# Every projection of a two-block model: 512 tokens per TensorE product, or two products of 256

## The chip, the cores and the metric

The kernel runs on one core of one Trainium2 chip. The metric is device microseconds of one execution, from launch to the last output. TensorE (PE in the rows) multiplies a stationary operand that a weight load (PEld) brings in by a moving operand of up to 512 columns, and writes to PSUM; VectorE (DVE) and ScalarE (ACT) empty PSUM and prepare operands, GpSimd (POOL) does small side work, SyncE (SP) issues the large loads.

## The reference

A sequence of 512 tokens of width 1024 goes through two blocks, all in float32:

```python
h = h + hybrid_mixer(rmsnorm(h))          # block 1: w_in projections, SSD, window attention, w_out
h = h + hierarchical_moe(rmsnorm(h))      # 64 experts, two per token
h = rmsnorm(h)
h = h + hybrid_mixer_2(rmsnorm_2(h))      # block 2: w_in projections, neighbourhood attention, GLA, w_out
u = rmsnorm_2(h) @ w_ff1                  # 1024 -> 4096
h = h + jnp.square(jax.nn.relu(u)) @ w_ff2
```

What the change touches is every product of the normed activations by a 128-column slice of an input weight: `proj = h @ w_in` in both mixers (all but a few narrow columns), and `u = ... @ w1` in the last feed-forward.

## The kernel before

Activations lie transposed: `A` is a pair of tiles of 128 partitions x 8 x 512 (features, tokens). To keep float32 accuracy with a faster product, each operand is split in two parts, a rounded one (H) and the remainder (L), and three products stand for one: H by H, H by L, L by H. `mm3` (L174) issues them, L178, L179 and L180:

```python
m = mm(out, lH, rH, start=first, stop=False)
mm(out, lH, rL, start=False, stop=False)
mm(out, lL, rH, start=False, stop=last)
```

`wsplit` (L152) splits a 128-column slice of a weight: ScalarE copies it rounded (`wH`, L158), VectorE subtracts (`wL`, L159). `proj` (L191) then makes one output slice of 128 features x 512 tokens in one PSUM bank of the pair tagged `pj`: 8 steps over the features, three products each, 24 products of 512 tokens. The weight part is the stationary operand, the activations are the moving one. The parameter `cuts` makes it go over the tokens in pieces, and is 2 for the first two slices of the feed-forward only (L1697). `late` (L1387, the first two value slices of block 2) issues all products with `wH` first, and those with `wL` behind.

There are 86 projections: 30 in block 1 (10 in `attention1`, 4 in `ssd_head`, 16 in `ssd`), 24 in block 2 (4 values, two of them `late`, 8 queries and keys, 8 + 4 in `gla`), 32 in `ffn`. Each is followed by VectorE or ScalarE work that reads the whole bank. Output projections (`wout`, `wout_tail`) also use `mm3`, with the weights as moving operand of 512 columns; `proj` is not in them. Between the blocks the experts stream their weights through SP's queue (L149).

The kernel is built through a framework that schedules: it puts the instructions of each engine into one fixed order by priorities and by its own estimate of when each is ready, and adds the waits. So an edit can also change where other instructions stand.

Of the kernel before, what the change touches and what calls it, by code (L numbers as in the profile page):

```python
# [15 lines left out]
P = 128  # L16
T = 512
# [11 lines left out]
class Net:  # L29
# [158 lines left out]
                                  start=True, stop=True)  # L188
        self.copy(out, p)

    def proj(self, W, A, m=P, cuts=1, late=False):  # L191

        p = self.psum("pj")
        kt = W[0].shape[1]
        if late:
            for k in range(3 * kt):
                w, a = ((0, 0), (0, 1))[k % 2] if k < 2 * kt else (1, 0)
                k, n = (k // 2 if k < 2 * kt else k - 2 * kt), k
                self.nc.tensor.matmul(p[:m], W[w][:, k, :], A[a][:, k, :], start=n == 0, stop=n == 3 * kt - 1)
            return p  # L200
        for c in range(cuts):
            ts = slice(c * (T // cuts), (c + 1) * (T // cuts))
            for k in range(kt):
                self.mm3(p[:m, ts], (W[0][:, k, :], W[1][:, k, :]), (A[0][:, k, ts], A[1][:, k, ts]), k == 0, k == kt - 1)
        return p
# [1165 lines left out]
    def neighbours(self, small, pool, wp, mixp, w_in, A):  # L1371
# [6 lines left out]
        W = []  # L1378
# [5 lines left out]
        for j in range(4):  # L1384
            if j > 1:
                W.append(self.wsplit(wp, wv[j], P))
            p = self.proj(W[j], A, P, late=j < 2)  # L1387
            self.copy(bycol(vT[:, j, :]), raster(p))

        row = self.dram.tile([1, T], FT, name="r2d")  # L1390
# [77 lines left out]
        for j in range(4):  # L1468
            now, ahead = ahead, project(j + 1) if j < 3 else None
            if j == 0:  # L1470

                v = []
                for n in range(7):
                    p = self.psum("tp")
# [210 lines left out]
    def ffn(self, pool, wp, A, r3):  # L1685
        nc, i, h = self.nc, self.ins, self.H
        V = nc.vector
        w1 = i["w_ff1_2"][0].rearrange("(k p) n -> p k n", p=P)
        w2 = i["w_ff2_2"][0].rearrange("(k p) n -> p k n", p=P)
        for q in range(4):  # L1690
            mixes = []
            for b in range(2):
                w = self.ring([P, KT, 512], w1[:, :, (2 * q + b) * 512:(2 * q + b + 1) * 512])
                m = self.mixtile(pool)
                mixes.append(m)
                for j in range(4):
                    p = self.proj(self.wsplit(wp, w[:, :, j * P:(j + 1) * P], P), A, P, 2 if q + b == 0 and j < 2 else 1)  # L1697
                    r = pool.tile([P, T], FT, name="r", bufs=2)
                    nc.scalar.activation(r, p, AF.Relu)
                    s = pool.tile([P, T], FT, name="s", bufs=2)  # L1700
                    V.scalar_tensor_tensor(s, p, 0.0, r, op0=OP.max, op1=OP.mult)
                    self.split(m[0][:, j, :], m[1][:, j, :], s)
            w = [self.ring([P, 4, D], w2[:, 8 * q + 4 * b:8 * q + 4 * b + 4, :]) for b in range(2)]
            srcs = lambda half, s: w[s // 2][:, 2 * (s % 2):2 * (s % 2) + 2, half * 512:half * 512 + 512]
            if q < 3:
                self.wout(wp, h, srcs, mixes, r3)
            else:
                self.wout(wp, h, srcs, mixes[:1], r3)
                g = self.row(pool, "ln_final_g_2")
                out = self.out[0].rearrange("(c p) d -> p c d", p=P)  # L1710
                self.wout_tail(self.tail_weights(wp, self.halves(self.mixtile(pool)), w[1]), h, mixes[1], r3,
                               lambda c: nc.sync.dma_start(out[:, c, :], self.normed(pool, h[:, c, :], g)))
# [114 lines left out]
```

## Time and profile before

| | us |
|---|---|
| median of 3 runs | 2036.48 (2032.88 to 2038.64) |
| profiled execution | 2035.26 |
| its span, first to last instruction | 2033.5 |
| TensorE busy | 1936.5 (95%) |
| VectorE / ScalarE busy | 948.4 / 534.1 |
| mean granted TensorE clock | 0.985 of full |

The span divides into five stages: loads and the first norm (to about 20 us), the mixer of block 1 (to 362), the tail of block 1, routing and experts (to 1340), the mixer of block 2 (to 1670) and the feed-forward (to the end). A row of the trace of one product gives its start and how long it takes from start to end; products overlap, so the time that one costs TensorE is the distance from its start to the next one's start, called a step below.

### The profile page before, as it was taken

What the parts mean: (1) busy time and instruction counts of PE and PEld (TensorE: products, weight loads), DVE (VectorE), ACT (ScalarE), POOL (GpSimd) and SP (SyncE); (2) the same over time, 40 slices, a digit from 0 to 9 for tenths busy, and PEclk for the clock granted to TensorE, in tenths of its full rate; (3) what the DMA queues carried; (4) which work ended last, traced back from release to release, by engine and by line L of the source; (5) the groups of instructions that cost most, each with busy time, mean ns of one, the idle gap of its engine ahead of it and who ended that gap; (6) DMA issues with size and microseconds to landing.
All of it is one profiled execution on the core that took longest, in us unless ns stands there. A gap on an engine that the chain in (4) does not pass through costs nothing. (4 is left out here: it accounts for less than half of the span.)

```text
span 2033.5 us, 24005 instructions
## 1 busy us (share of the span) xinstructions
PE 1936.5 (95%) x9535; PEld 1217.1 (60%) x9535; DVE 948.4 (47%) x1891; ACT 534.1 (26%) x899; POOL 192.1 (9%) x245
## 2 busy tenths in 40 slices
PE   7999999999999899999999999999999999999998
PEld 6788777734444344334344434447777778888886
DVE  6764657743543244243244333235655664443355
ACT  5773445311000010010010010024442433232232
POOL 5210333110000000000000000002201110000000
PEclk9999999999999999999999999999999999999999
DMA  7312012799999999999999999984212112313211
GB/s 203 115 43 83 27 70 111 259 342 415 415 424 426 424 424 424 424 424 425 424 424 424 422 422 424 422 320 68 91 42 83 43 52 83 118 50 123 99 68 42
DMA packets 114777, 494.24 MB, mean 243 GB/s; under 512 B 16492, under 2 KB 23091, under 8 KB 74984
## 3 DMA queue, kind: packets, MB, share of 16 engines
q1 hardware_dynamic: 107720, 483.63, 59.8%
q0 software_dynamic: 6352, 6.96, 1.5%
q10 hardware_dynamic: 592, 2.10, 0.3%
q8 instruction: 76, 1.25, 0.2%
q14 instruction: 37, 0.30, 0.0%
HBM read 500.68 MB, written 6.15 MB: 249 GB/s over the span
## 5 line engine op out<-in xcount | busy, mean ns | idle before, releaser
L986 PE MATMUL pj<-w,xg 128*64 128x512 f32 x1696 | 470.1, 608 | 45.9 <-DMA w<-in_w_up 45.2
L986 PEld LDWEIGHTS pj<-w,xg 128*64 128x64 f32 x1696 | 154.8, 140 | 332.2 <-issue 255.0
L159 DVE TENSOR_TENSOR wL<-w,wH 128x1024 fp32r<-128x1024 f32 x135 | 167.0, 1237 | 205.4 <-ACT wH L158 203.0
L158 ACT CAST wH<-w 128x1024 fp32r<-128x1024 f32 x136 | 142.4, 1048 | 343.4 <-PE pj L179 169.4
L1091 DVE SCALAR_TENSOR_TENSOR hid<-pj,slots,hid 128x512 f32<-128x512 f32 x30 | 22.5, 751 | 430.1 <-PE pj L986 415.8
L1190 DVE TENSOR_TENSOR H<-sc,H 128x512 f32<-128x512 f32 x248 | 156.6, 683 | 6.2 <-PE sc L1187 3.5
L986 PE MATMUL pj<-w16x,xg 128*64 128x512 f32 x352 | 151.7, 614 | 1.1 <-DMA w16x<-in_w_gate 1.1
L1187 PE MATMUL sc<-yH,ST 128*128 128x512 f32 x256 | 112.8, 441 | 0.6 <-DVE H L1190 0.6
L843 POOL DMA_INDIRECT rows<-hd,tok x31 | 31.7, 1022 | 815.1 <-DVE gates L837 576.3
L1100 ACT COPY hT<-tp 128x512 f32<-128x512 f32 x32 | 18.8, 587 | 339.8 <-PE tp L1098 339.8
L180 PE MATMUL pj<-n3H,wL 128*128 128x512 f32 (+1 forms) x272 | 103.6, 381 | 0.8 <-DVE wL L159 0.8
L178 PE MATMUL pj<-n3H,wH 128*128 128x512 f32 (+1 forms) x272 | 103.6, 381 | 0.0
L179 PE MATMUL pj<-n3L,wH 128*128 128x512 f32 (+1 forms) x272 | 103.5, 381 | 0.0
L178 PE MATMUL pj<-A,wH 128*128 128x512 f32 x240 | 97.6, 407 | 4.0 <-ACT wH L158 2.8
L1187 PE MATMUL sc<-yL,ST 128*128 128x512 f32 x252 | 100.0, 397 | 0.0
L179 PE MATMUL sc<-wL,mixH 128*128 128x512 f32 x252 | 99.2, 394 | 0.0
L178 PE MATMUL sc<-wH,mixH 128*128 128x512 f32 x252 | 99.1, 393 | 0.0
L180 PE MATMUL sc<-wH,mixL 128*128 128x512 f32 x252 | 98.8, 392 | 0.0
L179 PE MATMUL pj<-A,wH 128*128 128x512 f32 x240 | 97.4, 406 | 0.0
L180 PE MATMUL pj<-A,wL 128*128 128x512 f32 x240 | 96.7, 403 | 0.5 <-DVE wL L159 0.5
L986 PE MATMUL y<-w,hT 128*64 128x512 f32 x336 | 78.0, 599 | 0.6 <-DMA w<-in_w_down 0.6
L986 PE MATMUL tp<-w,hT 128*64 128x512 f32 x336 | 76.5, 592 | 0.0
(578 smaller groups left out, 3294.8 us busy)
## 6 DMA issues: line engine op xcount, KB each, us to landing
w<-in_w_up SPq DMA_DIRECT2D x88, 1024.0 KB, 20.8
w<-in_w_gate SPq DMA_DIRECT2D x84, 1024.0 KB, 19.6
w<-in_w_down SPq DMA_DIRECT2D x70, 1024.0 KB, 19.6
w16x<-in_w_down SPq DMA_DIRECT2D x32, 1024.0 KB, 20.2
w<-in_w_ff SPq DMA_DIRECT2D x16, 2048.0 KB, 8.1
w<-in_w_in SPq DMA_DIRECT2D x12, 2048.0 KB, 11.2
w<-in_w_up SPq DMA_DIRECT2D x40, 512.0 KB, 9.9
w16x<-in_w_gate SPq DMA_DIRECT2D x20, 1024.0 KB, 19.8
```

The costliest lines, as they stand in the source:

```text
L158: a = nc.scalar.copy(H, src)
L159: b = (engine or nc.vector).tensor_tensor(L, src, H.bitcast(FT), OP.subtract)
L178: m = mm(out, lH, rH, start=first, stop=False)
L179: mm(out, lH, rL, start=False, stop=False)
L180: mm(out, lL, rH, start=False, stop=last)
L843: self.nc.gpsimd.indirect_dma_start(out=rows, out_offset=None, in_=self.hd[:, :], in_offset=bass.IndirectOffsetOnAxis(ap=tok, axis=0), bou ...
L986: return self.pin(nc.tensor.matmul(*a, **k))
L1091: V.scalar_tensor_tensor(hid, pu, r, hid, op0=OP.mult, op1=OP.mult)
L1100: nc.scalar.copy(hT.rearrange("p j s -> p (j s)"), p)
L1187: m = nc.tensor.matmul(p, ST[:n, t * P:(t + 1) * P], y[:n], start=k == 0, stop=k == len(mms) - 1)
L1190: nc.vector.tensor_tensor(h[:, t, hs], p, h[:, t, hs], OP.add)
```

## The change

`proj` loses `cuts`; it always goes over the tokens in two pieces of 256, first all 24 products of tokens 0 to 255, then all 24 of tokens 256 to 511. In the `late` form the two pieces alternate under each weight part, so the same weight slice is used twice in a row. The two callers drop the parameter.

```diff
-    def proj(self, W, A, m=P, cuts=1, late=False):
+    def proj(self, W, A, m=P, late=False):
...
-                self.nc.tensor.matmul(p[:m], W[w][:, k, :], A[a][:, k, :], start=n == 0, stop=n == 3 * kt - 1)
+                for c in range(2):
+                    ts = slice(256 * c, 256 * c + 256)
+                    self.nc.tensor.matmul(p[:m, ts], W[w][:, k, :], A[a][:, k, ts], start=n + c == 0, stop=n + c == 3 * kt)
             return p
-        for c in range(cuts):
-            ts = slice(c * (T // cuts), (c + 1) * (T // cuts))
+        for c in range(2):
+            ts = slice(256 * c, 256 * c + 256)
             for k in range(kt):
                 self.mm3(p[:m, ts], (W[0][:, k, :], W[1][:, k, :]), (A[0][:, k, ts], A[1][:, k, ts]), k == 0, k == kt - 1)
...
-            p = self.proj(W[j], A, P, late=j < 2)
+            p = self.proj(W[j], A, P, j < 2)
...
-                    p = self.proj(self.wsplit(wp, w[:, :, j * P:(j + 1) * P], P), A, P, 2 if q + b == 0 and j < 2 else 1)
+                    p = self.proj(self.wsplit(wp, w[:, :, j * P:(j + 1) * P], P), A)
```

Two instructions of TensorE's queue (a weight load and a product) become four for each of 84 x 24 = 2016 products. Lines behind L202 move down by two. In the rows of order, a line is that of the source, then the operation, the tile written, the tiles read and the shape written; `A_90` and `A_91` are the H and L parts of `A`.

TensorE's queue at the first projection, the attention keys of block 1, whose products stand among the last transposes (L283, after: L285) of the norm. Before:

```order
L178 MATMUL pj<-A_90,wH 128x512
L283 MATMUL tp<-ident,xn 128x128 x4
L179 MATMUL pj<-A_91,wH 128x512
L180 MATMUL pj<-A_90,wL 128x512
L283 MATMUL sc<-ident,xn 128x128 x4
```

Now:

```order
L178 MATMUL pj<-A_90,wH 128x256
L285 MATMUL tp<-ident,xn 128x128 x4
L179 MATMUL pj<-A_91,wH 128x256
L180 MATMUL pj<-A_90,wL 128x256
L178 MATMUL pj<-A_90,wH 128x256
L285 MATMUL sc<-ident,xn 128x128 x4
```

Three products of 512 tokens stood ahead of the last four transposes, with 21 behind; now four of 256 tokens stand there, with 44 behind, of which the last 24 are the second piece of the tokens.

TensorE's queue in the attention of block 1, where the second pair of heads' probabilities is transposed (L525, after: L527) ahead of their product with the values (L531, after: L533). Before:

```order
L178 MATMUL pj<-A_90,wH 128x512
L179 MATMUL pj<-A_91,wH 128x512
L180 MATMUL pj<-A_90,wL 128x512
L525 MATMUL tp<-ident,S 128x128 x14
L531 MATMUL y<-PT,v 64x128
```

Now:

```order
L178 MATMUL pj<-A_90,wH 128x256
L527 MATMUL tp<-ident,S 128x128
L179 MATMUL pj<-A_91,wH 128x256
L527 MATMUL tp<-ident,S 128x128 x6
L180 MATMUL pj<-A_90,wL 128x256
...
L527 MATMUL tp<-ident,S 128x128 x7
L533 MATMUL y<-PT,v 64x128
```

The fourteen transposes that stood in one run now stand in three, with products of the next projection between them. In all, TensorE's queue has 85 runs of projection products in block 1 before and 90 now, 35 in block 2 either way; in `ffn` the queue is the same but for the cut.

## Rows read from the trace of the kernel before

**Rows 1.** The page: TensorE's and VectorE's busy time, share, instructions.

```profile
PE 1936.5 (95%) x9535; PEld 1217.1 (60%) x9535; DVE 948.4 (47%) x1891; ACT 534.1 (26%) x899; POOL 192.1 (9%) x245
```

**Rows 2.** Busy time by stage: stretch, length, each engine's busy us (instructions), clock, DMA.

```profile
40.00:362.00 322.00, 315.32 (x1793) 250.18 (x1792) 207.75 (x430) 179.54 (x355) 83.59 (x82) 0.99 0.21 72
362.00:1340.00 978.00, 924.47 (x4300) 412.45 (x4298) 367.83 (x830) 102.71 (x159) 40.50 (x53) 0.98 1.00 412
1340.00:1670.00 330.00, 314.34 (x1739) 241.93 (x1739) 189.29 (x371) 124.94 (x213) 48.10 (x72) 0.97 0.28 84
1670.00:2034.00 364.00, 353.95 (x1588) 290.30 (x1588) 159.13 (x201) 109.19 (x143) 1.88 (x2) 0.99 0.23 83
```

**Rows 3.** Lines L178 and L199: products, durations min/median/max ns, first and last start, forms.

```profile
L178 PE MATMUL pj<-n3H,wH x272: 276/394/399, 1670.4 to 1980.4; 128*128 128x512 f32 x120, 128*128 128x256 f32 x16
...
L178 PE MATMUL pj<-A,wH x240: 388/394/796, 15.5 to 361.3; 128*128 128x512 f32 x120
...
L178 PE MATMUL pj<-n2H,wH x176: 388/396/793, 1384.1 to 1623.9; 128*128 128x512 f32 x176
```

**Rows 4.** TensorE in order of time, feed-forward: start us, duration us, line, tiles, form.

```profile
1672.15 0.28 PE L180 MATMUL pj<-n3H,wL 128*128 128x256 f32 x1
...
1682.35 0.28 PE L180 MATMUL pj<-n3H,wL 128*128 128x256 f32 x1
1682.47 0.39 PE L178 MATMUL pj<-n3H,wH 128*128 128x512 f32 x1
1682.69 0.40 PE L179 MATMUL pj<-n3L,wH 128*128 128x512 f32 x1
...
1716.06 0.40 PE L178 MATMUL sc<-wH,mixH 128*128 128x512 f32 x1
```

**Rows 5.** The same view in block 1's attention, around one run of transposes.

```profile
59.66 0.39 PE L178 MATMUL pj<-A,wH 128*128 128x512 f32 x1
...
63.62 0.40 PE L180 MATMUL pj<-A,wL 128*128 128x512 f32 x1
63.92 1.23 PE L525 MATMUL tp<-ident,S 128*128 128x128 f32 x7
65.62 0.55 PE L525 MATMUL tp<-ident,S 128*128 128x128 f32 x3 [0.47 <-ACT PT L526]
```

**Rows 6.** The same view in block 2, a projection at half clock and then at full.

```profile
1619.68 0.63 PE L179 MATMUL pj<-n2L,wH 128*128 128x512 f32 x1
1620.11 0.63 PE L180 MATMUL pj<-n2H,wL 128*128 128x512 f32 x1
...
1622.00 0.40 PE L179 MATMUL pj<-n2L,wH 128*128 128x512 f32 x1
...
1624.34 0.40 PE L180 MATMUL pj<-n2H,wL 128*128 128x512 f32 x1
```

**Rows 7.** The same view, attention scores of block 1: other products of 256 columns.

```profile
124.24 1.59 PE L477 MATMUL sc<-kd,q 128*128 128x256 f32 x12
125.67 0.39 PE L180 MATMUL pj<-A,wL 128*128 128x512 f32 x1
```

**Rows 8.** The same view, the first projection, and VectorE's last split before it.

```profile
15.48 0.80 PE L178 MATMUL pj<-A,wH 128*128 128x512 f32 x1
...
20.89 0.40 PE L178 MATMUL pj<-A,wH 128*128 128x512 f32 x1
...
24.88 0.39 PE L180 MATMUL pj<-A,wL 128*128 128x512 f32 x1
...
20.82 0.74 DVE L172 SCALAR_TENSOR_TENSOR A<-sc,ca,A 128x512 fp32r<-128x512 f32 x1
```

**Rows 9.** TensorE's waits by releaser, total us, times, longest: block 1, experts, block 2.

```profile
PE pj L178 <- ACT wH L158: 2.8, 3, 1.0
...
PE pj L986 <- DMA w<-in_w_up: 45.2, 22, 3.7
...
PE tp L1622 <- DVE kd L1602: 5.0, 2, 4.3
PE y L1659 <- DVE st L1635: 3.1, 1, 3.1
```

**Rows 10.** SyncE's queue: what its loads waited for from 300 to 440 us.

```profile
SPq L149 <- DVE wL L159: 90.4, 4, 47.2
SPq L149 <- PE pj L986: 19.3, 8, 10.8
```

**Rows 11.** The page: the queue that brings instructions: packets, MB, share.

```profile
q8 instruction: 76, 1.25, 0.2%
```

## The prediction

> **What bounds the kernel now.** I read the page's busy times first: TensorE is busy for 1936.5 of 2033.5 us, VectorE for less than half [rows 1]. A share is an average, so the table by stage comes next [rows 2]: in the mixer of block 1 TensorE works 315 of 322 us, in that of block 2 314 of 330, in the feed-forward 354 of 364, the end of the kernel included. In these three stages TensorE is the limit, and in the experts' stage it is the transfers (412 GB/s, DMA share 1.00), which the change leaves alone. All 86 projections lie in the first, third and fourth stage. So the question is simple: what does TensorE pay for 512 tokens in one product, and what for two of 256?
>
> The duration of a product doesn't tell it. It is 394 ns at 512 tokens and 276 ns at 256 [rows 3], and by these two products would cost 552 ns for 394. But products overlap: the next starts long before the last has ended. What counts is the step from start to start, so I went to the rows in order of time, at the one place where both forms stand side by side: the feed-forward begins with two projections in two pieces and goes on with whole ones. The 91 products from 1672.15 to 1682.47 take 10.32 us, **113.4 ns each**; the 144 from there to the first output projection at 1716.06 take 33.59 us, **233.3 ns each** [rows 4]. Two products of 256 thus take 226.8 ns, 6.5 ns less than one of 512, with a weight load for each.
>
> **The change part by part.**
>
> *Products.* The line L178 has 240, 176 and 272 products for the three inputs, eight to a projection in one piece (the row of n3H lists its forms at half their count: 30 projections of 8 and two of 16) [rows 3]. That is 30 + 22 + 30 projections, with the two late ones of block 2 it makes 84 that change, of 24 products: 2016. If each gains what it would in the feed-forward, the sum is 2016 x 6.5 = **13.1 us**: 4.7 in the feed-forward (720), 4.7 in block 1 (720), 3.7 in block 2 (576). Is the step at 512 the same in the mixers? In block 1, 17 steps from 59.66 to 63.62 take 3.96 us, 232.9 ns [rows 5]; in block 2, 10 steps from 1622.00 to 1624.34 take 2.34 us, 234 ns [rows 6]. So yes for the half that is measured. The step at 256 has no row there; its bounds are 113.4 from the same code in the feed-forward, and 119.2 from other products of 256 columns, the attention scores of block 1, where twelve take 1.43 us from 124.24 to 125.67 [rows 7]. I take 113.4, since shape, tiles, order of operands and code are those of the changed ones, while the scores change their bank after every second product. The upper end is a rival below. Where the clock is at its lower level (the rows at 1619.68 and 1620.11 are 430 ns apart, against 234 behind [rows 6]) I count no gain; the mean clock of 0.97 to 0.99 in these stages makes that a few dozen products, 0.2 us at most.
>
> *Late form.* The 48 products of the two late projections now use each weight slice twice in a row. No row has that; between nothing saved and a full 6.5 ns on each, it is 0 to 0.3 us, and inside the sum already.
>
> *The first projection.* Its inputs arrive slice by slice, and the kernel before finished right behind them. Now the first piece follows the arrivals, and 24 products of the second piece, 24 x 113.4 = 2.7 us, can only start when the first piece is through. VectorE's last split of this input ends at 21.56; TensorE started its third step at 20.89 and was at its last product at 24.88 [rows 8], so it was the products, not the arrivals, that took the time. With six products of the first piece left behind the last arrival at worst (0.7 us), the second piece would end at about 21.6 + 0.7 + 2.7 = 25.0, where the last product ended its step at 25.1 before. On the good side, the four to six products that stood among the transposes are half as long. I put 0; the bounds are -1.3 and +2.
>
> *Order.* The scheduler was given other lengths, and the queue of block 1 has 90 runs of projection products for 85. A change between these products and others costs TensorE something: from the last product of a run to the transposes behind it 300 ns pass where a step is 233 [rows 5], and the way back costs about as much again. Five more runs at 0.1 us are **+0.5 us**. Against it, finer pieces fill holes: the 0.47 us before the transposes at 65.62 [rows 5], behind which ScalarE had to empty a bank, is just where products of 256 now stand between the transposes. In the feed-forward the queue is the same.
>
> *Waits.* What TensorE waits for in the mixers is short in all: the longest are 5.0 and 3.1 us in the linear attention of block 2, behind VectorE's recurrence, and 2.8 us behind ScalarE's weight copies [rows 9]. A wait whose releaser doesn't get faster eats the gain of the products just ahead of it. At most every such wait in the mixers swallows one projection's gain of 24 x 6.5 = 0.16 us; with some ten of them that is 1.6 us, and I take **+1.0**. What goes the other way, a last product that ends 118 ns after the others' step would, because 276 ns is less than 394 [rows 3], is of the same size and left in the range. VectorE and ScalarE don't become the limit: they are busy 65% and 56% of block 1's mixer, 44% and 30% of the feed-forward [rows 2].
>
> *Does block 1's gain survive the experts?* There TensorE waits 45.2 us for weights [rows 9]; a transfer that started no earlier would eat the 4.7 us. But its start hangs on block 1: from 300 to 440 us SyncE's queue waited for the weight splits 90.4 us and for TensorE 19.3 us [rows 10], and these come earlier with the projections. I count it whole and keep its loss as a rival.
>
> The sum: -13.1 + 0.2 + 0.5 + 1.0 = -11.4 us. The profiled execution took 2035.26 us (span 2033.5, the rest lies around it), so it would become 2023.9. The median of before is 1.2 us above it, which gives 2025.1; I say **2025**. A measurement of this kernel can tell about 0.3%, 6.1 us, from no change, so faster means below 2030.4 and slower above 2042.6.
>
> **The rivals.**
>
> *A, slower: each product has a fixed cost, and twice as many pay it twice.* Then a step of 256 isn't half of one of 512 but more, as it is at the attention scores, 119.2 ns [rows 7]: two make 238.4, 5.1 ns more than 233.3. On 2016 products that is +10.3 us, with the 1.5 of order and waits 2047. It decides from a step of 116.7 ns. For it speak the scores' rows, taken while ScalarE and VectorE are at their busiest; against it the 91 steps at 113.4 in a row, weight loads included, in the very same code [rows 4]. The Trainium skill, "TensorE: Matmul & The Clock Gate" (Wait — 56ns, not 53.3ns?), states this rule: a warm product costs its columns at 2.4 GHz and about 2.5 ns on top, whatever its size. By that page, as an estimate, 2016 more products would cost 5 us, and the kernel would take about 2041. By that rule the trace does not agree: here the larger product has the larger excess, 233.3 ns for 213.3 of columns against 113.4 for 106.7 [rows 4].
>
> *B, no change: the new order costs what the products save.* If one wait of about 1.2 us, like the longest of the others' 1.0 [rows 9], came in for half of the sixteen head and channel groups of block 1, 8 x 1.2 = 9.6 us would go: 2034.7. Against it speaks that most of the queue keeps its pattern; for it, that VectorE's and ScalarE's order in attention changed too, and no row shows those waits.
>
> *C, smaller gain: the transfers of the experts set their end.* Block 1's 4.7 us are waited away: 2029.7. The queue's releasers speak against it [rows 10].
>
> *D, no change: it doesn't do what it says, since TensorE can't be fed.* If instructions at double rate came too late, a pair would fall back to the 233 ns of before or worse: 2036 to 2040. The queue for instructions moved 1.25 MB in 76 packets in the whole run [rows 11], and these projections add a fifth to TensorE's 9535 products; the feed-forward would then issue 2308 products in about 360 us, 156 ns each, where the mixer of block 1 already issued 1793 in 322, 180 ns each [rows 2]. So it is near what was done before.
>
> **How the numbers follow.** Forecast 0.68, A 0.07, B 0.11, C 0.09, D 0.05. The forecast's own range is 2019 (everything counted, waits shrinking with it, two runs of luck in the order) to 2030; it and C lie almost whole on the faster side, and a part of the forecast's upper tail, 0.02, with B and D on the side of no change, with 0.01 of A. Faster 0.75, no change 0.19, slower 0.06. For 8 in 10 the range takes in C and the near half of B: 2018 to 2034.
>
> **What would show it.** Right: products of L180, L181 and L182 at 113 to 114 ns from start to start in all three stages, the feed-forward some 4.7 us shorter from its first projection to the end, block 1 and block 2 each about 4 us shorter, and the waits of TensorE there as before. Rival A shows as steps of 117 ns or more in block 1 alone; B as new rows in the table of waits, by VectorE or ScalarE; C as more than 45.2 us of waits for weights; D as holes between products that no engine ends. Wrong would be above all a step that holds in the feed-forward but not beside the busy engines of the mixers.

## The result, and the profile after

| | before | after |
|---|---|---|
| median, us | 2036.44 (2032.88 to 2038.64, 5 runs) | 2045.69 (2043.37 to 2048.25, 5 runs) |
| ratio after/before | | 1.0056, 95% interval 1.0044 to 1.0069 |
| profiled execution's span | 2033.5 | 2041.7 |

The change made the kernel slower, by about half a per cent: the medians differ by 9.3 us, the ratio of all runs makes it 11.4 (0.0056 x 2036.4). Below, "so many us more or less" means such a product of a ratio, unless medians are named. The prediction of 2025 with a range of 2018 to 2034 was wrong in its sign; rival A had said 2047.

The page after, in the columns of [rows 1] and [rows 11]:

```profile
PE 1943.1 (95%) x11551; PEld 1325.3 (65%) x11551; DVE 946.7 (46%) x1891; ACT 535.7 (26%) x901; POOL 191.9 (9%) x245
...
q8 instruction: 92, 1.51, 0.3%
```

TensorE has 2016 products more and is busy 6.6 us longer, where the sum had it 13 us shorter. Its busy share is 95% as before, and by stage it is still what sets the time, as in [rows 2]:

```profile
40.00:362.00 322.00, 316.57 (x2420) 286.03 (x2419) 205.27 (x428) 177.42 (x353) 82.13 (x81) 1.00 0.21 72
362.00:1340.00 978.00, 924.57 (x4305) 411.40 (x4305) 368.48 (x833) 103.52 (x160) 40.94 (x52) 0.98 1.00 411
1340.00:1670.00 330.00, 313.55 (x2305) 273.48 (x2302) 184.74 (x365) 124.40 (x211) 47.19 (x72) 0.97 0.28 87
1670.00:2034.00 364.00, 361.58 (x2347) 329.70 (x2345) 162.13 (x201) 111.43 (x146) 3.37 (x4) 1.00 0.22 81
```

Where it was lost is read from the first and last start of the line L178 for the three inputs, beside [rows 3]:

```profile
L178 PE MATMUL pj<-n3H,wH x512: 275/281/363, 1678.2 to 1988.9; 128*128 128x256 f32 x171
...
L178 PE MATMUL pj<-A,wH x480: 273/282/415, 15.6 to 365.2; 128*128 128x256 f32 x160
...
L178 PE MATMUL pj<-n2H,wH x352: 276/281/416, 1387.5 to 1634.3; 128*128 128x256 f32 x176
```

In this pair of profiles block 1 begins at the same time and ends 3.9 us later (365.2 for 361.3; the last experiment shows that the pair understates it). The experts hand 3.4 of that on (1387.5 for 1384.1), block 2 adds 4.4 (the feed-forward begins at 1678.2 for 1670.4), and the feed-forward next to nothing (310.7 us between its two marks for 310.0). It should have gained 4.7.

The steps tell why. TensorE in order of time, as in [rows 4]; in each pair of rows the products between first and last all have one form, with no idle time: 32 steps in block 1, 34 in block 2, then 147 in the feed-forward's first quarter and 188 in its second (the "..." stand for them):

```profile
59.82 0.29 PE L179 MATMUL pj<-A,wH 128*128 128x256 f32 x1
...
63.66 0.28 PE L178 MATMUL pj<-A,wH 128*128 128x256 f32 x1
...
1559.75 0.28 PE L179 MATMUL pj<-n2L,wH 128*128 128x256 f32 x1
...
1563.77 0.28 PE L180 MATMUL pj<-n2H,wL 128*128 128x256 f32 x1
...
1699.74 0.28 PE L180 MATMUL pj<-n3H,wL 128*128 128x256 f32 x1
...
1716.40 0.28 PE L180 MATMUL pj<-n3H,wL 128*128 128x256 f32 x1
...
1773.81 0.28 PE L180 MATMUL pj<-n3H,wL 128*128 128x256 f32 x1
...
1795.95 0.28 PE L179 MATMUL pj<-n3L,wH 128*128 128x256 f32 x1
```

That is 3.84 us / 32 steps = **120.0 ns** in block 1, 4.02 / 34 = **118.2** in block 2, 16.66 / 147 = **113.3** in the first quarter, and 22.14 / 188 = **117.8** in the second; the third and fourth quarters repeat the second. The prediction's 113.4 is right for the stretch from which it was read, and for no other. Against 233.3 for a whole product, two products cost 240.0, 236.4, 226.6 and 235.6. One instruction, one form, the same code gives four steps, each steady through its stretch. So the question for the experiments was: what sets the step?

Three theories: **places**, the step depends on where in SBUF the two operands lie; **history**, what came just before a stretch sets it; **neighbours**, ScalarE and VectorE at work beside it raise it. Beside these, rival B: that the order of instructions takes part of the loss.

### The profile page after: what moved, and what is told of

Its sections match the earlier page's. It is cut to its first block, busy times and chain, and to the rows that moved or that the text cites. A ratio compares the mean times of both kernels' runs of the same rounds, so it can differ in the third digit from the quotient of the medians.

```text
span 2041.7 us, 28049 instructions
## 1 busy us (share of the span) xinstructions
PE 1943.1 (95%) x11551; PEld 1325.3 (65%) x11551; DVE 946.7 (46%) x1891; ACT 535.7 (26%) x901; POOL 191.9 (9%) x245
## 4 chain that ended last, share of the span: by engine, by line
PE 58%; DMA 30%; DVE 6%; ACT 4%; issue 1%; POOL 0%; SPq 0%; DVEq 0%; ACTq 0%; POOLq 0%
DMA w<-in_w_up 16%; PE pj L988 10%; PE pj L179 7%; PE pj L180 7%; PE pj L178 7%; DMA w<-in_w_gate 7%; DMA w<-in_w_down 3%; DMA w16x<-in_w_down 3%; PE sc L179 3%; PE sc L180 3%; PE sc L178 3%; PE sc L1189 2%; PE y L988 1%; PE tp L988 1%; DMA w16x<-in_w_up 1%; DVE M L699 1%
## 5 line engine op out<-in xcount | busy, mean ns | idle before, releaser
L180 PE MATMUL pj<-n3H,wL 128*128 128x256 f32 x512 | 143.5, 280 | 0.8 <-DVE wL L159 0.8
L178 PE MATMUL pj<-n3H,wH 128*128 128x256 f32 x512 | 143.5, 280 | 0.0
L179 PE MATMUL pj<-n3L,wH 128*128 128x256 f32 x512 | 143.4, 280 | 0.0
L178 PE MATMUL pj<-A,wH 128*128 128x256 f32 x480 | 138.0, 288 | 2.0 <-ACT wH L158 1.0
L179 PE MATMUL pj<-A,wH 128*128 128x256 f32 x480 | 137.9, 287 | 0.0
L180 PE MATMUL pj<-A,wL 128*128 128x256 f32 x480 | 137.0, 285 | 0.8 <-DVE wL L159 0.8
L178 PE MATMUL pj<-n2H,wH 128*128 128x256 f32 x352 | 102.5, 291 | 0.0
L179 PE MATMUL pj<-n2L,wH 128*128 128x256 f32 x352 | 102.3, 291 | 0.0
L180 PE MATMUL pj<-n2H,wL 128*128 128x256 f32 x352 | 102.0, 290 | 0.0
L178 PE MATMUL sc<-wH,mixH 128*128 128x512 f32 x252 | 98.5, 391 | 0.0
```

## The experiments

For the first three kernels `proj` got a number of pieces that each stage sets (`self.cuts`, 1 or 2). Of two-piece projections: all 32 of the feed-forward; those of block 1; those of block 2's mixer.

```diff
+        cuts = cuts or self.cuts
-                for c in range(2):
-                    ts = slice(256 * c, 256 * c + 256)
+                for c in range(cuts):
+                    ts = slice(T // cuts * c, T // cuts * (c + 1))
```

**The feed-forward alone.** Expected: 

> Two pieces in all 32 projections of the feed-forward, everything else as before; TensorE's order stays that of before. The prediction's theory (a step of 113.4 ns for 256 columns in the feed-forward): 720 products x 6.5 ns = 4.7 us less, about 2032. The theory of a step that depends on the stretch (113.3 in the first quarter, 117.8 in the three behind it, as in the trace of the changed kernel): 180 x 6.6 = 1.2 us less there, 540 x 2.3 = 1.2 us more behind, so within 0.5 us of before, with the steps seen again in the same quarters.

Measured: ratio 0.9998 (0.9986 to 1.0011), no change. L178 shows the same stretch as before, 310.6 us from first to last start where [rows 3] has 310.0:

```profile
L178 PE MATMUL pj<-n3H,wH x512: 276/281/364, 1669.9 to 1980.5; 128*128 128x256 f32 x171
```

TensorE's order is that of before here, so the miss of 4.7 us is the step's alone. The steps are seen again in the same places: in this trace the feed-forward's first quarter has 113.4 ns and the other three have 117.8.

**Block 1 alone.** Expected: 

> Two pieces in the projections of block 1 only. If the step alone matters (119.06 ns in the changed kernel's trace against 233.34 for a whole product): 720 x 4.8 ns = 3.4 us more, 2040. If the new order costs as well, as the marks of the changed kernel say (4.6 us behind at the routing): about 4.5 us more. The prediction's theory (113.4) would give 4.7 us less.

**Block 2 alone.** Expected: 

> Two pieces in the projections of block 2's mixer only. If the step alone matters (118.31 against 233.19): 576 x 3.4 ns = 2.0 us more, 2038.5. If the new order of the linear attention's second half costs too, as the marks of the changed kernel say (3.4 us behind, then 10.1 at the mixer's last product, then 7.7): 4 to 5 us more, and the loss lies behind the neighbourhood attention. The prediction's theory would give 3.7 us less.

Measured: 1.0034 (1.0022 to 1.0045) and 1.0021 (1.0010 to 1.0031), that is 6.9 and 4.3 us. With the feed-forward's -0.4 they add up to 10.8, about what the whole change costs (11.4). Each mixer loses by itself. (The 119.06 of the first expectation lies below the 120.0 of undisturbed rows; with 120.0 block 1's steps give 4.8.) The line L178, block 1's kernel first, then block 2's:

```profile
L178 PE MATMUL pj<-A,wH x480: 274/282/388, 15.6 to 365.9; 128*128 128x256 f32 x160
...
L178 PE MATMUL pj<-n2H,wH x176: 388/396/793, 1387.5 to 1625.6; 128*128 128x512 f32 x176
```

```profile
L178 PE MATMUL pj<-n2H,wH x352: 274/281/415, 1384.6 to 1630.0; 128*128 128x256 f32 x176
L178 PE MATMUL pj<-n3H,wH x272: 276/394/398, 1673.5 to 1983.5; 128*128 128x512 f32 x120, 128*128 128x256 f32 x16
```

Block 1's 4.6 us (365.9 for 361.3) are still 3.4 us at block 2's first product (1387.5 for 1384.1): the transfers of the experts hide little of it, which speaks against rival C. In the second kernel block 2 begins 0.5 late (1384.6) and the feed-forward 3.1 late (1673.5 for 1670.4), so block 2 adds 2.6.

**TensorE by itself.** A small kernel does nothing but such products, in stretches, with the weights shifted by `o` elements of 4 bytes (`stall` makes TensorE wait some 2.4 us for VectorE):

```python
for o in (0, 8, 16, 32, 64, 128, 256, 512):
    stall(o)
    stretch(f"whole{o}", o, 512, 2)
    stretch(f"half{o}", o, 256, 3)
    stall(o)
    stretch(f"fresh{o}", o, 256, 3)
```

Expected: 

> Leaves out the whole model: TensorE alone multiplies stretches of 48 products of 512 columns, 144 of 256 without a stall before them, then 144 behind a stall of some us by VectorE, with the weights at eight distances of 32 to 2048 bytes from one place; then 144 of 256 that use each weight slice twice in a row, and 192 of 128. Nothing else runs. Theory of a fixed cost for each product (rival A): one step for all stretches of 256, 118 to 119 ns. Theory of history (what came just before the stretch sets how loads and products interleave): the stretch behind a stall has 113.3 and the one without 118, whatever the weights' place. Theory of addresses: the step goes with the weights' place, both stretches alike. Theory of neighbours (ScalarE and VectorE at work raise the step in the mixers): 113.3 everywhere.

TensorE in order of time; a stretch's step is the distance to the next row's start by its count. First `half` at shift 0, then `half` and `fresh` at 64 bytes:

```profile
28.77 17.43 PE L57 MATMUL half<-A,W 128*128 128x256 f32 x144
46.04 0.40 PE L57 MATMUL fresh<-A,W 128*128 128x256 f32 x2
...
131.24 17.12 PE L57 MATMUL half<-A,W 128*128 128x256 f32 x144
148.20 0.40 PE L57 MATMUL fresh<-A,W 128*128 128x256 f32 x2
150.99 16.38 PE L57 MATMUL fresh<-A,W 128*128 128x256 f32 x142 [2.39 <-DVE W L41]
167.21 0.62 PE L57 MATMUL whole<-A,W 128*128 128x512 f32 x2
```

17.27 / 144 = 119.9 ns at shift 0; 16.96 / 144 = 117.8 at 64 bytes, and 16.22 / 142 = 114.2 behind the stall there (113.4 without the slower steps at its start). No other engine worked beside these stretches, so neighbours are not needed for a slow step, and a fixed cost doesn't give three values. At shifts of 0, 256, 512, 1024 and 2048 bytes whole products have 227 and halves 120; at 32, 64 and 128 bytes they have other steps. So places count, and a shift by a multiple of 256 bytes changes nothing; at 64 bytes there are two states.

**The remaining distances, and what is relative to what.** The same kernel with shifts of 96, 160, 192 and 224 bytes; then the inputs moved by 64 bytes as well (`ao=16`), with the weights moved along or left:

```python
stretch("bothwhole", 16, 512, 2, ao=16)
stretch("bothhalf", 16, 256, 3, ao=16)
stretch("backwhole", 0, 512, 2, ao=16)
stretch("backhalf", 0, 256, 3, ao=16)
```

Expected: 

> Leaves out the whole model, as in the first run of stretches. There the step went with the weights' place relative to the inputs', modulo 256 bytes: 227 ns whole and 120 half at distance 0; 233.3 and 118.3 at 32 bytes; 233.3 and 113.3 or 117.8 at 64; 232.4 and 118.6 at 128. This run adds 96, 160, 192 and 224 bytes, then moves the inputs by 64 bytes: with the weights moved by 64 too (bothwhole, bothhalf), and with the weights left (backwhole, backhalf). If only the distance counts, both... gives 227 and 120, back... the steps of 192 bytes. If the absolute place of the weights counts, both... gives 233.3 and 113.3 or 117.8. At 160 bytes, the distance of block 1, 233.3 and 119.1 are expected. Then at 64 bytes, stretches of 256 behind a stall (one, six), behind whole products (three), behind quarters (five) and behind whole products at distance 0 (eight): if a stall sets the better of two states, one and six have 113.3 and the others 117.8.

```profile
234.21 17.44 PE L59 MATMUL bothhalf<-A,W 128*128 128x256 f32 x144
251.48 11.15 PE L59 MATMUL backwhole<-A,W 128*128 128x512 f32 x48
262.47 16.48 PE L59 MATMUL backhalf<-A,W 128*128 128x256 f32 x144
278.79 0.40 PE L59 MATMUL one<-A,W 128*128 128x256 f32 x2
281.57 16.99 PE L59 MATMUL one<-A,W 128*128 128x256 f32 x142 [2.38 <-DVE W L42]
298.40 11.36 PE L59 MATMUL two<-A,W 128*128 128x512 f32 x48
309.60 16.50 PE L59 MATMUL three<-A,W 128*128 128x256 f32 x144
325.94 10.83 PE L59 MATMUL four<-A,W 128*128 128x128 f32 x96
336.60 16.55 PE L59 MATMUL five<-A,W 128*128 128x256 f32 x144
```

And from 360 to 374 us alone, past the start of `six`, which also stands behind a stall:

```profile
359.80 13.76 PE L59 MATMUL six<-A,W 128*128 128x256 f32 x120
373.39 0.86 PE L59 MATMUL seven<-A,W 128*128 128x512 f32 x3
```

Moved together the step is 17.27 / 144 = 119.9, as unmoved: the distance counts, not the place of either. Left behind, at 192 bytes, it is 113.3 (16.32 / 144). History does not set the step alone, since at 0, 32 and 128 bytes the stretches behind a stall and those without one agree. It does not explain the two states at 64 bytes either, in the form put here: `one`, behind a stall, has 118.5 (16.83 / 142; 117.8 past its start), but `six`, behind a stall too, has 113.3 (13.59 / 120); `three`, behind whole products, has 113.5, but `half` in the run before had 117.8 there; `five` has 113.8 and `eight` 117.8. A stall does not pick the better state, and what does stays open. The table has the steps of the small kernels at full clock, in ns, the halves in the two stretches of each distance. Beside them stand the parts of the model that have this distance by the addresses that the build assigned (start of the stationary operand minus start of the moving one, modulo 256 bytes):

| distance, bytes | whole | half | in the kernel before and after |
|---|---|---|---|
| 0 | 227 | 120.0, 119.9 | output projections of block 1 and feed-forward; attention scores |
| 32 | 233.3 | 118.3, 118.3 | block 2's projections and three quarters of its output projection |
| 64 | 233.3 | 117.8, 113.4 | feed-forward's projections |
| 96 | 234.3 | 118.7, 117.3 | |
| 128 | 232.4 | 118.6, 118.7 | |
| 160 | 233.3 | 120.0, 120.0 | block 1's projections |
| 192 | 229 | 113.3, 117.8 | |
| 224 | 233.3 | 117.8, 117.8 | |

Every step of the changed kernel agrees with its line: 120.0, 118.2, and the feed-forward's two. Two halves at best cost 226.7, what one whole product costs at distance 0; at none of these distances less. And the kernel before holds the same evidence, in output projections, which are products of 512 too: 105 of them without a break in the feed-forward, from the row at 1716.06 in [rows 4], and 52 in block 2:

```profile
1493.66 0.40 PE L179 MATMUL tp<-wL,mixH 128*128 128x512 f32 x1
...
1505.79 0.40 PE L180 MATMUL tp<-wH,mixL 128*128 128x512 f32 x1
...
1739.88 0.39 PE L178 MATMUL sc<-wH,mixH 128*128 128x512 f32 x1
```

23.82 / 105 = 226.9 ns at distance 0, 12.13 / 52 = 233.3 at 32.

**Moving the weights in the model.** Small unused tiles of 96, 32 and 192 bytes bring the projections' weights to distance 0 from their inputs in all stages; TensorE's order does not change. Once for the kernel before, once for the changed one:

```diff
                 small = ctx.enter_context(tc.tile_pool(name="small1", bufs=1, reuse_waits="tile"))
+                small.tile([P, 24], FT, name="pad", bufs=1)
...
+            right = ctx.enter_context(tc.tile_pool(name="pad2", bufs=1, side="right", reuse_waits="tile"))
+            right.tile([P, 8], FT, name="pad")
...
             wp = ctx.enter_context(tc.tile_pool(name="wsp3", bufs=2, reuse_waits="tile"))
+            wp.tile([P, 48], FT, name="pad", bufs=1)
```

Expected, whole products: 

> The kernel before, with small unused tiles (96, 32 and 192 bytes per partition) that move the projections' weights to distance 0 modulo 256 bytes from their inputs, in all three stages; TensorE's order is that of before. Theory of places: 2016 whole products at 226.7 in place of 233.3 give 13.3 us, less 0.6 for the feed-forward's 96 products of 256 that go from 113.4 to 120: about 2024, less what waits take of it. Rival (history or neighbours set the step): no change, 2036.

Expected, halves: 

> The changed kernel with the same unused tiles; TensorE's order is that of the changed kernel. Theory of places: every step of 256 becomes 120, a pair 240; against the changed kernel's 238.1, 236.6, 226.6 and 235.6 in its stretches that is 720 x 1.9 + 576 x 3.4 + 180 x 13.4 + 540 x 4.4 = 8.1 us more, 2054, and 27 us plus the order's cost more than whole products at the same places. Rival: no change, 2046.

Measured: whole products 2027.44, ratio 0.9960 (0.9947 to 0.9972), faster by 8.1 us; halves 2050.73, 1.0068 (1.0054 to 1.0081), slower by 13.8. The step of the first kernel in the feed-forward (80 steps between its two rows), then the second's (184 steps):

```profile
1689.64 0.39 PE L178 MATMUL pj<-n3H,wH 128*128 128x512 f32 x1
...
1707.77 0.39 PE L180 MATMUL pj<-n3H,wL 128*128 128x512 f32 x1
```

```profile
1699.83 0.28 PE L180 MATMUL pj<-n3H,wL 128*128 128x256 f32 x1
...
1721.91 0.28 PE L178 MATMUL pj<-n3H,wH 128*128 128x256 f32 x1
```

226.6 and 120.0, as the table says, and the feed-forward takes 305.8 and 315.7 us from first to last start where it took 310.0 and 310.6:

```profile
L178 PE MATMUL pj<-n3H,wH x272: 282/389/396, 1662.6 to 1968.4; 128*128 128x512 f32 x120, 128*128 128x256 f32 x16
```

```profile
L178 PE MATMUL pj<-n3H,wH x512: 277/283/364, 1682.6 to 1998.3; 128*128 128x256 f32 x171
```

With these unused bytes and nothing else added to both kernels, the same split costs 21.9 us in place of 11.4 (by the medians 23.3 in place of 9.3). That places set the step in the model is shown. The gain of 8.1 falls short of the 12.7 expected. In the mixers the steps of this trace, leaving out those over some 250 ns, average 228.8 (block 1) and 227.8 (block 2) rather than 226.7, since the first steps of a run of products stay longer (past the sixth, in long runs, they are 227.0 and 226.7); this takes 2.1 us off (720 x 2.1 ns and 576 x 1.1). The traces show where it is missing: the feed-forward gained 4.2 us and block 2 3.0 (283.3 us from its first L178 to the feed-forward's, for 286.3). Block 1, which was to gain 4.8, has its last L178 at 356.7 us here and at 358.9 in the next kernel, where two traces with its old steps and the same granted clock have 358.1 and 357.9 (shown below): next to nothing, as far as two traces can tell. The halves miss the 2054 expected: its sum counts 720 x 1.9 ns for block 1, whose step was at 120.0 already, and what is left of the miss is inside the interval.

**Block 2's output projection too.** A further unused tile of 192 bytes in `small2`. Expected: 

> As the kernel before with distance 0 for the projections, and the mixed values of block 2 moved as well (192 bytes), so that block 2's output projection stands at distance 0 too, like those of the other stages, where its products take 226.7 in place of 233.1: some 144 to 190 products x 6.4 = 0.9 to 1.2 us on top of the projections' gain, 2023, if nothing waits there.

Measured: 2025.71, 0.9957 (0.9944 to 0.9969). That cannot be told from the kernel before it. Its median is the lowest of all the kernels here, 9.6 us under that of before measured beside it (2035.28), and it keeps whole products.

**Order or step?** The steps account for 720 x 6.7 ns = 4.8 us in block 1, 576 x 3.1 = 1.8 in block 2 and, in the feed-forward, 576 x 2.3 - 144 x 6.7 = 0.4: 7.0 of the 11.4. To see whether the new order is the rest, the changed kernel was built with TensorE's queue held in the order of before, by edges between each product and its predecessor from a table of runs:

```diff
+        for a, n in table:
+            for u in units[a:a + n]:
+                for x in u:
+                    if last is not None:
+                        self.tc.add_manual_dep(x, last.name, mybir.DependencyInfo(
+                            mybir.DependencyClass.NoSync, mybir.DependencyReason.DATA), reason="order")
+                    last = x
```

Expected: 

> The changed kernel, every projection in two pieces, but TensorE's queue held in the order of before: where one product of 512 stood, two of 256 stand, and nothing else is moved (126 runs of projection products in the whole queue, as before, where the changed kernel has 131). The weights stay where they were. If only the step counts (119.06, 118.31, and in the feed-forward 113.3 and 117.8): 720 x 4.8 + 576 x 3.4 + 0.3 = 5.8 us over before, about 2042, and what the changed kernel loses beyond that is its order's. If the order costs nothing, this kernel takes as long as the changed one, 2046.

And beside it the changed kernel as it is: 

> The changed kernel once more, beside the run before this one on the same chip, so that the order's share is their difference: 3 to 4 us if the step alone gives 5.8, none if the order costs nothing. Against before, 1.0044 to 1.0069 was measured first.

Measured: 2045.92, 1.0061 (1.0048 to 1.0074), and 2046.61, 1.0058 (1.0046 to 1.0070). The two agree within their intervals: the order costs nothing that can be measured here (less than some 3 us would not be seen). Nor does the trace of the first gain at the end of block 1, 367.0 where the changed kernel had 365.2 (the line L178 is L228 there):

```profile
L228 PE MATMUL pj<-A,wH x480: 274/282/579, 15.5 to 367.0; 128*128 128x256 f32 x160
```

**Where in block 2?** Two pieces in the neighbourhood attention's 12 projections alone, then in the linear attention's 12 alone (`self.cuts` set between the two). Expected: 

> Two pieces in the 12 projections of block 2's neighbourhood attention only. The steps alone (118.33 for 256, 233.19 whole): 288 x 3.5 = 1.0 us over before. All of block 2 in two pieces took 4.7 us more in the mean of its runs where its steps give 2.0; if the rest of 2.7 us lies here, 3.7 us; if it lies in the linear attention, 1.0.

> Two pieces in the 12 projections of block 2's linear attention only. The steps alone: 1.0 us over before. If the rest of 2.7 us lies here, where VectorE's recurrence makes TensorE wait and the granted clock falls most, 3.7 us; if it lies in the neighbourhood attention, 1.0. If it comes of half-clock stretches that fall at random, the two need not add up to 4.7 and differ by less than their intervals.

Measured: 1.0017 (1.0006 to 1.0028) and 1.0016 (1.0007 to 1.0025), 3.5 and 3.3 us. The steps give 288 x 3.1 ns = 0.9 each, and the intervals (1.2 to 5.7, 1.4 to 5.1) lie just above it. So the rest sits in no one place of block 2. What it is stays open: the steps explain 7.0 us, the one profiled pair differs by 8.1 (2043.37 against 2035.26), the timed runs by 11.4 with an interval of 9.0 to 14.1. The granted clock does not tell the kernels apart: it is 0.983 to 0.987 in the runs of the changed kernel measured again, and the same in those of before beside them.

Where it lies can be narrowed down with all the traces, which also shows how little one pair of profiles can tell. Block 1 has the same queue in five of them. Its last L178 starts at 361.3, 361.7 and 361.2 us in before, in block 2 alone and in linear attention alone, where the granted clock is 0.99 from 20 to 356 us, and some 3 us earlier in feed-forward alone and neighbourhood attention alone, where it is 1.00:

```profile
L178 PE MATMUL pj<-A,wH x240: 388/394/792, 15.6 to 358.1; 128*128 128x512 f32 x120
...
L178 PE MATMUL pj<-A,wH x240: 388/394/796, 15.6 to 357.9; 128*128 128x512 f32 x120
```

The four kernels with block 1 in two pieces at the old places (365.2, 365.9, 367.0, 365.1) all have 1.00. At an equal clock block 1 so loses 7 to 9 us where its steps give 4.8; a good part of the rest lies there, outside the undisturbed steps, and its cause was not found. The timed runs of block 1 alone (6.9) and block 2 alone (4.3, where the steps give 1.8) say the same: some 2 us of the rest in each mixer, none in the feed-forward.

## Why the prediction was wrong

**What bounds the kernel: right.** TensorE's busy time is near the whole of the three stages after as before, and a change of its step moves the whole in both directions: shorter steps of whole products at distance 0 gave 0.9960, longer ones of halves 1.0056 and, at distance 0, 1.0068. For block 1 there is a limit: it passed its longer steps on, but of the shorter ones next to nothing arrived.

**Products: wrong, and this is the step that failed.** "I take 113.4, since shape, tiles, order of operands and code are those of the changed ones". Code and shape do not fix the step; it goes with the distance of the operands. The two numbers of [rows 4] came from the one stretch in which 256 columns were in their best state, 113.3, while 512 columns stood at a distance where they have their worse step, 233.3. That difference of 6.5 ns a pair was multiplied by all 2016 products. It held for 144. In block 1 a pair cost 6.7 ns more than a whole product, in block 2 3.1 more, in the rest of the feed-forward 2.3 more, so that the term of -13.1 us was +7.0. The prediction's sign for being wrong, a step that holds in the feed-forward but not beside the busy engines of the mixers, missed as well: three quarters of the feed-forward did not have the step either, and no busy engine was needed. "Is the step at 512 the same in the mixers?" was rightly answered with yes, and told nothing about 256: at distances of 32, 64 and 160 bytes whole products all have 233.3 (table), so the half that could be measured was just the one that does not tell the stages apart.

The other bound was the right one for block 1. The attention scores at 119.2 [rows 7] were set aside "since the scores change their bank after every second product". They stand at distance 0, where 120 is the step of the small kernel. The bank is not the reason: the small kernel's stretches write to different banks, and at distance 0 all have 120.

**Rival A: right in its time by luck, wrong in its reason.** 2047 forecast, 2045.7 measured (the 1.2 us that the forecast adds for the median would make A's sum 2048). A priced the steps at 10.3 us and order and waits at 1.5; the steps cost 7.0, and 4.4 are of unknown cause. A fixed cost for each product would give one step for each width. There are 113.3 to 120.0 ns at 256 columns and 226.7 to 234 at 512, by distance, with two states at 64 and 192 bytes. The Trainium skill, "TensorE: Matmul & The Clock Gate" (Wait — 56ns, not 53.3ns?), has a fixed 2.5 ns on top of the columns; as an estimate by that page of the Trainium skill 256 columns would take 109.2 ns and 512 would take 215.8. No stretch in these runs comes as low as either.

**Late form, first projection: right, and small.** Using a slice twice in a row saves nothing; each product still has its own weight load (11551 of each in the page after), and in the small kernel `pair` at distance 0 has 120, like `half`. The first projection's last product starts at 25.01, against 24.88 in [rows 8] for one that is twice as long: no loss, as put.

```profile
25.01 0.28 PE L180 MATMUL pj<-A,wL 128*128 128x256 f32 x1
```

**Order, +0.5, and waits, +1.0: not disproved, perhaps too small.** Order is 0 within an error of some 3 us by the run that held it (2045.92 against 2046.61). The waits of the mixers are much as in [rows 9]; the longest in block 2:

```profile
PE tp L1624 <- DVE kd L1604: 5.2, 2, 4.4
PE y L1661 <- DVE M L1650: 3.8, 3, 2.6
```

Some 4.4 us (11.4 less 7.0) may stand where these terms were; only their sum, not its cause, was seen. What such terms take from a true gain is seen in the kernel with whole products at distance 0: of 12.7 us of shorter steps 8.1 arrived (interval 5.7 to 10.8). Of the 4.6 lost, 2.1 are steps that did not become that short, which the sum had no term for; the other 2.5 stand beside its 1.5 for order and waits. Rival B's 9.6 us did not come, with the new order or without it.

**C and D: rightly set aside.** What block 1 lost came through the experts. In the twelve traces of the model the last L178 of block 1 starts between 356.7 and 368.1 us, a spread of 11.4, and the first of block 2 between 1379.3 and 1389.1, a spread of 9.8. C's sign, more than 45.2 us of waits for weights, did not come either: 45.0 in the trace after. Instructions were not the limit: 92 packets for 76, and 188 products in a row without a gap at 117.8 ns.

**What was overlooked in the profile.** [rows 4] ended with the first output projection, and behind it stood 105 products of 512 columns at 226.9 ns, while block 2's had 233.3. One form with two steps, both steady, in the trace of before: that said that form and code do not determine the step, and so that 113.4 could not be carried to another stage. The chance of 0.07 for A should have been far larger.

## What to carry over

A step read in one place holds for that place: before multiplying it by thousands, look for a second stretch of the same form elsewhere in the trace, and if the two differ, find out what differs (here the operands' addresses) before forecasting. When the bounds of a term have opposite signs, as 113.4 and 119.2 had around the break-even of 116.7, the row nearest in code is not enough to choose. And before splitting or merging products, try moving their operands: 320 unused bytes per partition gained 8 us where splitting all projections lost 11.

## What the runs showed of the hardware

TensorE's step for products of this kernel's kind (float32 in its rounded form, 128 x 128 weights, full clock) depends on the distance of the stationary operand's address from the moving one's, and is the same when that distance grows by 256, 512, 1024 or 2048 bytes. Distances were tried in steps of 32 bytes. At 512 columns it is 227 ns at distance 0, 229 at 192 and 232.4 to 234.3 elsewhere. At 256 columns other distances are good and bad: 120 at 0 and 160, 117.3 to 118.7 at most others. At 64 and 192 bytes 256 columns have two states, 113.3 and 117.8, each of which lasts through a stretch; neither a stall nor whole products ahead decide which. At 128 columns and 64 bytes the step is 111 ns (`four`, 10.66 us / 96), hardly less than at 256. Why the distance sets the step stays open.
